# A hybrid decoder layer on one core: gates and branch products turned to token-major, and two late loads cut into pieces

## The chip, the cores and the metric

One core of one Trainium2 chip. The metric is the device time of one launch in microseconds, lower is better. The kernel before was run three times: median 1575.02 us (1573.05 to 1575.83).

## What is computed

The layer reads 256 tokens of width 2048. One input projection feeds three branches (dilated attention A, chunked gMLP B, an S5 state-space layer C) and three gates per channel; each branch is projected back to 2048, weighted by its gate, summed, and projected once more; a SwiGLU feed-forward part follows. Cut to what matters here:

```python
proj = x @ w_in + b_in                       # x: 256 x 2048
q, k, v, zb, uc, gl = split(proj)            # gl: 3 x 2048 gate columns
ya = ...                                     # attention, 512 wide
yb = ...                                     # gMLP, 768 wide
yc = gelu(s5(uc))                            # scan over 256 tokens
yc = yc * sigmoid(yc @ w_glu + b_glu)        # 768 wide
gates = sigmoid(gl.reshape(256, 3, 2048))
merged = gates[:, 0] * (ya @ w_pa) + gates[:, 1] * (yb @ w_pb) + gates[:, 2] * (yc @ w_pc)
x = layer_norm(ALPHA * x + merged @ w_o, ln1_g, ln1_b)
gate_f, up = split(x @ w_ffn_in)
f = (silu(gate_f) * up) @ w_ffn_out
out = layer_norm(ALPHA * x + f, ln2_g, ln2_b)
```

## The kernel before

**Number format.** Everything is float32 in and out. For TensorE a float32 value is split into a high part h (rounded to fp32r, by ScalarE: L280 for weights) and a low part l (the rest, by VectorE: L299), and a product is made of three: high by high, low by high, high by low.

**Units.** The work is a list of units, each one block of weights (up to 128 x 1024) with its load, its split, its matmuls (`mm`) and, at the end of a group, an eviction (`post`). A loop at the end of the kernel writes them out in order. Ahead of a unit's matmuls it splits the weights of later units and issues their loads on SyncE's queue (SP): four raw buffers, four split buffers, so that the loads run about four units ahead and the splits up to four. All weight loads, and most of the others, go through that one queue in this order. Between units it steps generators (`spawn`): the S5 set-up and scan, attention, gMLP, the turning of the feed-forward's rows (`turns`). `later` puts a small piece of work off by a unit.

**Feature-major stages** (`wide`, L80): the weights are the stationary operand, 128 output features at a time, and the activations are the moving one. `xT` holds per k 256 tokens of high and 256 of low part, so one matmul of 512 columns (L85: h by high and low) and one of 256 (L86: l by high) make a pair; 16 k make a tile of 128 features by 256 tokens. The two halves of the bank are added on eviction: ScalarE takes one half with the bias (L357, one value per partition), VectorE adds the other (L359).

**Token-major stages** (`tall`, L165; V, the output projection and the last projection): 128 tokens of activations are stationary, and 512 weight columns move, three matmuls (L171 to L173) per k and token half, and two banks (one per token half) for a group of 512 features.

**Gates and branch products before.** There are 16 feature tiles f and three branches b. `gates(f, b)` (L1312) is a wide group of two units; its eviction leaves 128 x 256 in `gx` (b of 0 or 1) or `g2` (b of 2), and a tanh a unit later (L887). `p_unit(f, b)` (L897) multiplies the branch's output by its projection, feature-major, with three matmuls of 256 columns per k (L906 to L908; 4, 6 and 6 k). Its eviction (L916, L918) multiplies by the gate and adds into `mab`, which is feature-major as well; for b of 2 the add is GpSimd's and the sum is split into `m` (high and low), as the output projection wants it: features on partitions.

**The scan.** Branch C's recurrence runs on GpSimd in two blocks of 128 time steps, four instructions a step (L586 to L589), on the tile X. The first block runs from about 100 us, the second beside the gates. `s5_out(1)` reads X on TensorE (L600); it is spawned at unit Y1, seven units before the first unit of the GLU (L1364).

**The last projection.** Its first unit's `before` is `ln2_load` (L1277): it starts the last `turns`, and issues four loads on SP: the residual rows `z` (two of 1 MB, kept in DRAM until then) and the norm weights `ln2w` (two of 1 MB, broadcast to the partitions). They go into the buffers that the seven-product stage's sums and `x1T` held.

The stages by time: input projection with q and k to 193 us, V to 259, gMLP inputs to 353, gates and products of branches 0 and 1 to about 611, the rest of the gates with the GLU to 711, the products of branch 2 to 746, output projection to 835, feed-forward to 1314, last projection to the end.

Of the kernel before, what the change touches and what calls it, by code (L numbers as in the profile page):

```python
# [32 lines left out]
def hybrid_layer(ctx: ExitStack, tc: tile.TileContext, d: dict, out: bass.AP):  # L33
# [24 lines left out]
    def s6(shape, dt, name):  # L58
        return sb.tile(shape, dt, tag="s6", bufs=11, name=name)
# [115 lines left out]
    def tall(srcs, kk, n, act, post, before=None, late=None, homes=()):  # L175
# [25 lines left out]
        for u, src in enumerate(srcs):  # L201
            last = u == len(srcs) - 1
            units.append(Unit(src, kk, n, mk(u), (lambda: post(st["ps"])) if last and not late else None,
                              before if u == 0 else None,
                              uses=1 if u < first_held else HL_BUFS if last else 0,
                              home=homes[u - first_held] if 0 <= u - first_held < len(homes) else None))

# [19 lines left out]
    def later(fn, wait=1):  # L227

        deferred.append([fn, wait])
# [16 lines left out]
    with tc.manual_schedule():  # L246
# [400 lines left out]
        def tables():  # L647
# [11 lines left out]
            for blk in range(4):  # L659
# [13 lines left out]
                yield  # L673
            s1 = dram.tile([8, L_TAB], F32, name="tab1")
# [198 lines left out]
        def gate(f, b):  # L873

            if b < 2:
                return big["gx"][:, f % 6, :]
            return big["g2", f // 6][:, f % 6, :]

        def post_gate(f, b):
# [16 lines left out]

        def p_unit(f, b, before=None):  # L897
            k0, k1 = ((0, 4), (4, 10), (10, 16))[b]
            st = {}

            def mm(h, l):
                st["ps"] = o = bank()[:, 0:256]
                for j in range(k1 - k0):
                    a = act_p(k0 + j)
                    hs, ls = h[:, j * 128:(j + 1) * 128], l[:, j * 128:(j + 1) * 128]
                    T.matmul(o, lhsT=hs, rhs=a[:, 0:256], start=j == 0, stop=False)  # L906
# [3 lines left out]
            def post():  # L910
                if (f, b) == (0, 0):
                    big["mab"] = sb.tile([128, 16, 256], F32, tag="t16", bufs=1, name="mab")
                if b == 2 and f % 3 == 0:
                    big["m", f // 3] = s6([128, 3, 512], F32R, f"m{f // 3}")
                g, m = gate(f, b), big["mab"][:, f, :]
                V.scalar_tensor_tensor(g if b else m, g, 1.0, st["ps"], op0=ALU.add, op1=ALU.mult)  # L916
                if b:
                    (G if b == 2 else V).tensor_tensor(m, m, g, op=ALU.add)  # L918
                if b == 2:
                    y = big["m", f // 3][:, f % 3, :]  # L920
                    later(lambda: copy_split(y[:, 0:256], y[:, 256:512], m))

            units.append(Unit(d["w_p"][f, :, k0:k1, :].rearrange("p k c -> p (k c)"), k1 - k0, 128, mm, post, before))
# [219 lines left out]
        def three(ps, a, h, l, start, stop):  # L1143
            T.matmul(ps, lhsT=a[0], rhs=h, start=start, stop=False)  # L1144
            T.matmul(ps, lhsT=a[1], rhs=h, start=False, stop=False)  # L1145
            T.matmul(ps, lhsT=a[0], rhs=l, start=False, stop=stop)  # L1146

# [129 lines left out]
        def ln2_load():  # L1277
            big["z"] = sb.tile([128, 2, D], F32, tag="t16", bufs=1, name="z")
            for t in range(2):
                nc.sync.dma_start(big["z"][:, t, :], big["zd"][:, t, :])  # L1280
            w = sb.tile([128, 2, D], F32, tag="t32", bufs=1, name="ln2w")
            spawn(turns(LAST))
            for i, nm in enumerate(("ln2_g", "ln2_b")):
                nc.sync.dma_start(w[:, i, :], d[nm].partition_broadcast(128))
            big["ln2"] = w
# [26 lines left out]
        def gates(f, b):  # L1312
            wide(wb(30 + f if b == 2 else 52 + 2 * f + b), 8, actx, post_gate(f, b))

# [5 lines left out]
        gates(0, 0)  # L1320
        for b in range(2):
            for f in range(16):
                if f < 15:
                    gates(f + 1, b)
                else:
                    gates(0, b + 1)
                p_unit(f, b, (lambda: finish(marks["gmlp"])) if (f, b) == (0, 1) else None)
        for f in range(1, 14):
            gates(f, 2)
# [3 lines left out]
        for f in range(14, 16):  # L1333
            gates(f, 2)
        for f in range(16):
            p_unit(f, 2)
# [225 lines left out]
```

## Time and profile before

| | |
|---|---|
| median of three runs | 1575.02 us |
| the profiled execution's own time | 1573.56 us |
| its span, first to last instruction | 1571.8 us |
| granted TensorE clock, mean | 0.997 |
| TensorE busy | 1546.5 us (98%), 8474 matmuls |
| VectorE / ScalarE / GpSimd busy | 1034.5 / 767.6 / 560.8 us |
| moved by DMA | 311.63 MB, mean 198 GB/s |

A row of a group reads: line, engine, operation, out<-in by the program's names, shapes, count | busy us, mean ns of one | idle time before and what ended it. A row of the timeline: start us, duration us, engine, line, operation. Matmuls overlap in the records, since one starts before the end of the one before it is written down; the distance between two starts tells what one costs in a dense stretch. SPq rows are the issue of transfers, not the transfers.

### The profile page before, as it was taken

To read this page: it belongs to the slowest core of one execution; us is meant where nothing else is said; L and a number is where in the kernel's file an instruction comes from. 1 tells how busy PE (TensorE), PEld (TensorE's weight loads), DVE (VectorE), ACT (ScalarE), POOL (GpSimd) and SP (SyncE) were. 2 spreads that over 40 slices of the span, in tenths; PEclk is the share of its full clock that TensorE was granted. 3 is DMA by queue.
4 is the path that set the end of the run, shared out by engine and by line. 5 is a ranking of instruction groups with operands and counts; after the bars stand their busy time and mean duration, and the time that the engine had idled before them with its cause. 6 is when DMAs were issued, how large, how long until landed. Compare 5 with 4: busy or idle time off the path is not lost.

```text
span 1571.8 us, 23107 instructions
## 1 busy us (share of the span) xinstructions
PE 1546.5 (98%) x8474; PEld 1322.4 (84%) x8474; DVE 1034.5 (66%) x1318; ACT 767.6 (49%) x990; POOL 560.8 (36%) x1149
## 2 busy tenths in 40 slices
PE   8999999999999999999999999999999999999996
PEld 6888888898889998889889888888888887788885
DVE  5444555666856665469567788888888886555455
ACT  5454443556444444465444555555555554433342
POOL 7549999963999999303003000000000000000002
PEclk9999999999999999999999999999999999999998
DMA  7665565666665556556883666666666667666663
GB/s 277 202 222 187 188 217 174 179 184 188 209 193 185 187 188 199 187 155 182 292 286 131 195 190 212 187 193 197 189 199 189 189 201 290 207 195 192 197 190 105
DMA packets 168505, 311.63 MB, mean 198 GB/s; under 512 B 27631, under 2 KB 110063, under 8 KB 167624
## 3 DMA queue, kind: packets, MB, share of 16 engines
q1 hardware_dynamic: 168008, 307.92, 61.8%
q0 software_dynamic: 384, 2.25, 0.4%
q8 instruction: 66, 1.08, 0.3%
q14 instruction: 47, 0.39, 0.1%
HBM read 305.87 MB, written 7.63 MB: 199 GB/s over the span
## 4 chain that ended last, share of the span: by engine, by line
PE 91%; DVE 4%; DMA 2%; ACT 1%; issue 1%; POOL 0%; SPq 0%; POOLq 0%; ACTq 0%; DVEq 0%
PE ps_mm L85 21%; PE ps_mm L86 11%; PE ps_mm L171 8%; PE ps_mm L172 8%; PE ps_mm L173 8%; PE ps_sd L1146 5%; PE ps_sd L1144 4%; PE ps_mm L1144 4%; PE ps_mm L1146 4%; PE ps_sd L1145 4%; PE ps_mm L1145 4%; DVE wl L299 2%; PE ps_mm L908 1%; PE ps_mm L907 1%; PE ps_mm L906 1%; DMA raw<-in_w_f_dram 1%
## 5 line engine op out<-in xcount | busy, mean ns | idle before, releaser
L280 ACT ACTIVATE wh<-raw 128x1024 fp32r<-128x1024 f32 (+1 forms) x544 | 556.1, 1025 | 471.6 <-PE ps_mm L173 163.3
L299 DVE TENSOR_TENSOR wl<-raw,wh 128x1024 fp32r<-128x1024 f32 (+1 forms) x544 | 654.7, 1225 | 146.6 <-ACT wh L280 144.3
L85 PE MATMUL ps_mm<-xT,wh 128*128 128x512 f32 x1344 | 481.9, 401 | 7.7 <-ACT wh L62 5.7
L86 PE MATMUL ps_mm<-xT,wl 128*128 128x256 f32 x1344 | 378.8, 282 | 0.4 <-DVE wl L299 0.4
L85 PEld LDWEIGHTS ps_mm<-xT,wh 128*128 128x128 f32 x1344 | 253.9, 189 | 70.3 <-ACT wh L62 5.7
L987 POOL TENSOR_TENSOR z<-z,ln2w 128x512 f32<-128x512 f32 (+1 forms) x4 | 5.2, 1297 | 709.0 <-ACT z L986 709.0
L86 PEld LDWEIGHTS ps_mm<-xT,wl 128*128 128x128 f32 x1344 | 255.5, 190 | 1.3 <-DVE wl L299 0.7
L586 POOL TENSOR_TENSOR t<-s5keep,X 128x48 f32<-128x48 f32 x254 | 131.8, 519 | 50.7 <-ACT X L568 30.9
L589 POOL TENSOR_TENSOR X<-X,t 128x48 f32<-128x48 f32 x255 | 130.2, 511 | 20.0
L172 PE MATMUL ps_mm<-wl,h 128*128 128x512 f32 x340 | 132.4, 389 | 2.2 <-DVE wl L299 2.2
L171 PE MATMUL ps_mm<-wh,h 128*128 128x512 f32 x340 | 132.6, 390 | 0.4 <-ACT wh L280 0.4
L173 PE MATMUL ps_mm<-wh,h 128*128 128x512 f32 x340 | 132.3, 389 | 0.0
L588 POOL TENSOR_TENSOR X<-X,t 128x48 f32<-128x48 f32 x255 | 119.3, 468 | 32.8 <-ACT X L568 32.8
L587 POOL TENSOR_TENSOR t<-s5keep,X 128x48 f32<-128x48 f32 x254 | 111.7, 440 | 0.0
L357 ACT ACTIVATE tmp<-ps_mm,bcol 128x256 f32<-128x256 f32 x90 | 42.8, 475 | 137.9 <-PE ps_mm L86 137.7
L1144 PE MATMUL ps_sd<-wh,x1T 128*128 128x512 f32 x270 | 106.1, 393 | 0.0
L1144 PE MATMUL ps_mm<-wh,x1T 128*128 128x512 f32 x270 | 105.9, 392 | 0.0
L1146 PE MATMUL ps_sd<-wl,x1T 128*128 128x512 f32 x270 | 105.4, 390 | 0.0
L1146 PE MATMUL ps_mm<-wl,x1T 128*128 128x512 f32 x270 | 105.2, 390 | 0.0
L1145 PE MATMUL ps_mm<-wh,x1T 128*128 128x512 f32 x270 | 105.1, 389 | 0.0
L1145 PE MATMUL ps_sd<-wh,x1T 128*128 128x512 f32 x270 | 105.1, 389 | 0.0
L172 PEld LDWEIGHTS ps_mm<-wl,h 128*128 128x128 f32 x340 | 63.8, 188 | 15.6 <-DVE wl L299 2.6
(277 smaller groups left out, 2475.2 us busy)
## 6 DMA issues: line engine op xcount, KB each, us to landing
raw<-in_w_f_dram SPq DMA_DIRECT2D x264, 512.0 KB, 4.1
raw<-in_w_b_dram SPq DMA_DIRECT2D x164, 512.0 KB, 4.8
raw<-in_w_o_dram SPq DMA_DIRECT2D x32, 512.0 KB, 5.3
raw<-in_w_v_dram SPq DMA_DIRECT2D x24, 512.0 KB, 3.9
raw<-in_w_p_dram SPq DMA_DIRECT2D x32, 384.0 KB, 3.5
raw<-in_w_zv_dram SPq DMA_DIRECT2D x16, 384.0 KB, 3.6
tmp<-tab SPq DMA_DIRECT2D x64, 64.0 KB, 2.8
raw<-in_w_p_dram SPq DMA_DIRECT2D x16, 256.0 KB, 3.3
```

The lines of the kernel that those rows point to most:

```text
L85: T.matmul(ps, lhsT=h[:, j * 128:(j + 1) * 128], rhs=a, start=k == 0, stop=last, skip_group_check=True)
L86: T.matmul(ps[:, 0:256], lhsT=l[:, j * 128:(j + 1) * 128], rhs=a[:, 0:256], start=False, stop=last, skip_group_check=True)
L171: T.matmul(ps[:, :n], lhsT=ah, rhs=hs, start=k == 0, stop=False)
L172: T.matmul(ps[:, :n], lhsT=ah, rhs=ls, start=False, stop=False)
L173: T.matmul(ps[:, :n], lhsT=al, rhs=hs, start=False, stop=k == total - 1)
L280: A.activation(h[:, :m], raws[n][:, :m], AF.Copy)
L299: V.tensor_tensor(l[:, :m], raws.pop(n)[:, :m], h[:, :m].bitcast(F32), op=ALU.subtract)
L586: G.tensor_tensor(t1, keep[:, 0], prev, op=ALU.mult)
L589: G.tensor_tensor(cur, cur, t2, op=ALU.add)
L1144: T.matmul(ps, lhsT=a[0], rhs=h, start=start, stop=False)
L1145: T.matmul(ps, lhsT=a[1], rhs=h, start=False, stop=False)
L1146: T.matmul(ps, lhsT=a[0], rhs=l, start=False, stop=stop)
```

## The change

Gates and branch products become token-major, by groups n of four feature tiles (512 columns). `two_tiles` makes the units: a unit holds two k of four feature tiles, and each k and token half t takes three matmuls of 512 columns into one of two banks. `gates(n, b)` has 8 units, `p_units(n, b)` 2 or 3. The weight arrays are laid out as before, so a load takes four runs of two k (1 KB a run) where it took one run of eight.

The bias can no longer be a value per partition. `tables` turns the bias columns once on TensorE and writes them to DRAM as 96 rows (`rows`); the first unit of each gate group loads its four rows, broadcast to all partitions, into a free third of `gx` or a temporary; the eviction is one VectorE add per token half, and the tanh follows at once on ScalarE. `mab` is token-major, so after the products of branch 2 `turn_m` turns each 512 columns, four transposes per token half, on TensorE, and splits them into `m`. The order of the units of the third branch changes too: 24 gate units before the GLU (28 before), 8 after it between the first products. Y1 stays at seven units before the GLU.

`ln2_load` now only allocates; the loads go out in 12 pieces of 512 columns, one every three units, by the generator `load_late`.

```diff
+        def two_tiles(srcs, act, post, before=None):
...
+                    if u == 0:
+                        st["ps"] = [bank(), bank()]
+                    for t in range(2):
+                        for j in range(2):
+                            a = act(2 * u + j)
+                            hs, ls = (w.rearrange("p (f k c) -> p k f c", f=4, k=2)[:, j] for w in (h, l))
+                            three(st["ps"][t], (a[:, t * 128:(t + 1) * 128], a[:, 256 + t * 128:256 + (t + 1) * 128]),
+                                  hs, ls, (u, j) == (0, 0), (u, j) == (len(srcs) - 1, 1))
...
+        def gates(n, b):
...
+                row["b"] = tmp() if b == 2 else big["gx"][:, 2, :]
+                src = big["rows"][f0:f0 + 3 * fs + 1:fs, :]
+                nc.sync.dma_start(row["b"].rearrange("p (f c) -> p f c", f=4),
+                                  src.unsqueeze(0).to_broadcast([128, 4, 128]))
+
             def post(ps):
-                if (f, b) == (0, 0):
-                    big["gx"] = s6([128, 6, 256], F32, "gx")
-                if b == 2 and f % 6 == 0:
-                    big["g2", f // 6] = s6([128, 6, 256], F32, f"g2{f // 6}")
-                s = gate(f, b)
-                add_bias(ps, (C_G2 + f) if b == 2 else C_G01 + 2 * f + b, s)
-                later(lambda: A.activation(s, s, AF.Tanh, scale=0.5))
-            return post
+                for t in range(2):
+                    V.tensor_tensor(gate(n, b, t), ps[t], row["b"], op=ALU.add)
+                for t in range(2):
+                    A.activation(gate(n, b, t), gate(n, b, t), AF.Tanh, scale=0.5)
...
+        def p_units(n, b, before=None):
+            k0, k1 = ((0, 4), (4, 10), (10, 16))[b]
+
+            def post(ps):
+                if (n, b) == (0, 0):
+                    big["mab"] = sb.tile([128, 2, D], F32, tag="t16", bufs=1, name="mab")
+                for t in range(2):
+                    g, m = gate(n, b, t), big["mab"][:, t, n * 512:(n + 1) * 512]
+                    V.scalar_tensor_tensor(g if b else m, g, 1.0, ps[t], op0=ALU.add, op1=ALU.mult)
+                    if b:
+                        (G if b == 2 else V).tensor_tensor(m, m, g, op=ALU.add)
+                if b == 2:
+                    spawn(turn_m(n))
...
+        def turn_m(n):
+
+            for t in range(2):
+                yield
+                ps = bank("sd")
+                for f in range(4):
+                    T.transpose(ps[:, f * 128:(f + 1) * 128],
+                                big["mab"][:, t, (4 * n + f) * 128:(4 * n + f + 1) * 128], ident)
...
-        def p_unit(f, b, before=None):
...
-                    T.matmul(o, lhsT=hs, rhs=a[:, 0:256], start=j == 0, stop=False)
-                    T.matmul(o, lhsT=hs, rhs=a[:, 256:512], start=False, stop=False)
-                    T.matmul(o, lhsT=ls, rhs=a[:, 0:256], start=False, stop=j == k1 - k0 - 1)
...
+        def load_late():
+
+            for g in range(4):
+                c = slice(g * 512, g * 512 + 512)
+                pieces = [(big["z"][:, :, c], big["zd"][:, :, c])]
+                pieces += [(big["ln2"][:, i, c], d[nm][c].partition_broadcast(128))
+                           for i, nm in enumerate(("ln2_g", "ln2_b"))]
+                for dst, src in pieces:
+                    for _ in range(3):
+                        yield
+                    nc.sync.dma_start(dst, src)
...
+        for n in range(3):
+            units.extend(gates(n, 2))
         marks["glu"] = len(units)
         for c in range(6):
             glu(c)
-        for f in range(14, 16):
-            gates(f, 2)
-        for f in range(16):
-            p_unit(f, 2)
+        last = gates(3, 2)
+        units.extend(last[0:3])
+        units.extend(p_units(0, 2))
+        units.extend(last[3:6])
+        units.extend(p_units(1, 2))
+        units.extend(last[6:8])
+        for n in (2, 3):
+            units.extend(p_units(n, 2))
```

What stands in the engines' lists is shown at three places. On TensorE, where the first gate group ends and the first product of branch 0 begins, before (`ya` is attention's output, `wh` and `wl` the split weights, L564 is the scan's input product):

```order
L85 MATMUL ps_mm<-xT,wh 128x512
L86 MATMUL ps_mm<-xT,wl 128x256
L564 MATMUL ps_sd<-uT,bbT 128x128 x8
L906 MATMUL ps_mm<-ya_2804,wh 128x256
L907 MATMUL ps_mm<-ya_2804,wh 128x256
L908 MATMUL ps_mm<-ya_2804,wl 128x256
```

and after the change:

```order
L209 MATMUL ps_mm<-wh,xT 128x512
L210 MATMUL ps_mm<-wh,xT 128x512
L211 MATMUL ps_mm<-wl,xT 128x512
L209 MATMUL ps_mm<-wh,ya_2810 128x512
L210 MATMUL ps_mm<-wh,ya_2810 128x512
L211 MATMUL ps_mm<-wl,ya_2810 128x512
```

The pair of 512 and 256 columns and the three of 256 have become three of 512 in both.

On VectorE, around the first reads of the second scan block (L603 before, L608 after, which take what TensorE made of X), in the gates of the third branch. Before (L359 is the add that ends one gate tile, L299 a weight split; `g_7218` holds tiles 6 to 11):

```order
L359 TENSOR_TENSOR g_7218<-ps_mm,tmp_7317 128x256
L299 TENSOR_TENSOR wl<-raw,wh 128x1024 x2
L359 TENSOR_TENSOR g_7218<-ps_mm,tmp_7366 128x256
L299 TENSOR_TENSOR wl<-raw,wh 128x1024 x2
L359 TENSOR_TENSOR g_7218<-ps_mm,tmp_7415 128x256
L603 SCALAR_TENSOR_TENSOR uT<-uT,bcol,ps_sd 128x4x32 x2
```

and after (L932 ends a gate group for one token half, L304 is the split):

```order
L932 TENSOR_TENSOR g_6178<-ps_mm,tmp_6179 128x512 x2
L304 TENSOR_TENSOR wl<-raw,wh 128x1024 x8
L932 TENSOR_TENSOR g_6178<-ps_mm,tmp_6332 128x512
L932 TENSOR_TENSOR g_6331<-ps_mm,tmp_6332 128x512
L304 TENSOR_TENSOR wl<-raw,wh 128x1024 x2
L608 SCALAR_TENSOR_TENSOR uT<-uT,bcol,ps_sd 128x4x32 x2
```

Before, the read comes with the eleventh gate tile of the branch (22 units of the branch); after, two units into the third group (18 units).

On SP's queue, where the last projection begins, before (`raw` are weight loads):

```order
L262 DMA raw<-in_w_f_dram 128x1024 x7
L1280 DMA z<-zd 128x2048 x2
L1284 DMA ln2w<-in_ln_g_dram 128x2048
L1284 DMA ln2w<-in_ln_b_dram 128x2048
L262 DMA raw<-in_w_f_dram 128x1024 x81
```

and after:

```order
L267 DMA raw<-in_w_f_dram 128x1024 x10
L1343 DMA z<-zd 128x2x512
L267 DMA raw<-in_w_f_dram 128x1024 x3
L1343 DMA ln2w<-in_ln_g_dram 128x512
L267 DMA raw<-in_w_f_dram 128x1024 x3
L1343 DMA ln2w<-in_ln_b_dram 128x512
```

The four large transfers, with 81 weight loads behind them, have become twelve with three weight loads between each.

More of the change, by code (lines that the diff above doesn't have):

```diff
@@ L206, in tall, with three @@
                               home=homes[u - first_held] if 0 <= u - first_held < len(homes) else None))
+    def three(ps, a, h, l, start, stop):
+        T.matmul(ps, lhsT=a[0], rhs=h, start=start, stop=False)
+        T.matmul(ps, lhsT=a[1], rhs=h, start=False, stop=False)
+        T.matmul(ps, lhsT=a[0], rhs=l, start=False, stop=stop)
     tasks = []
@@ L673, in tables @@
                 yield
+            ps = bank("sd")
+            T.transpose(ps[0:96, 0:128], bcol, ident)
+            rows = tmp(128)[0:96]
+            V.tensor_copy(rows, ps[0:96, 0:128])
+            big["rows"] = dram.tile([96, 128], F32, name="rows")
+            nc.sync.dma_start(big["rows"], rows)
             s1 = dram.tile([8, L_TAB], F32, name="tab1")
@@ new lines, in four, with mk, mm @@
+        def four(w, f0, fs, k0):
+            return w[f0:f0 + 3 * fs + 1:fs, :, k0:k0 + 2, :].rearrange("f p k c -> p f (k c)")
+        def two_tiles(srcs, act, post, before=None):
+            st = {}
+            def mk(u):
+                def mm(h, l):
+                    if u == 0:
[6 more added lines that the diff above has]
+                                  hs, ls, (u, j) == (0, 0), (u, j) == (len(srcs) - 1, 1))
+                return mm
+            return [Unit(src, 8, 128, mk(u), (lambda: post(st["ps"])) if u == len(srcs) - 1 else None,
+                         before if u == 0 else None) for u, src in enumerate(srcs)]
@@ L895, in act_p @@
             return act_yc2(k - 10)
-        def p_unit(f, b, before=None):
[L898 to L906, printed above, removed]
-                    T.matmul(o, lhsT=hs, rhs=a[:, 256:512], start=False, stop=False)
-                    T.matmul(o, lhsT=ls, rhs=a[:, 0:256], start=False, stop=j == k1 - k0 - 1)
[L910 to L923, printed above, removed]
         def act_m(k):
@@ L1277, in ln2_load @@
         def ln2_load():
+            spawn(turns(LAST))
             big["z"] = sb.tile([128, 2, D], F32, tag="t16", bufs=1, name="z")
[L1279 to L1285, printed above, removed]
+            big["ln2"] = sb.tile([128, 2, D], F32, tag="t32", bufs=1, name="ln2w")
+            spawn(load_late())
+        def load_late():
[8 more added lines that the diff above has]
+                    nc.sync.dma_start(dst, src)
         def ln2_norm(eng, t, c, n, part=None):
@@ L1319, in hybrid_layer @@
         marks["a"] = len(units)
-        gates(0, 0)
         for b in range(2):
-            for f in range(16):
[L1323 to L1328, printed above, removed]
-            gates(f, 2)
+            for n in range(4):
+                units.extend(gates(n, b))
+                units.extend(p_units(n, b, (lambda: finish(marks["gmlp"])) if (n, b) == (0, 1) else None))
+        for n in range(3):
+            units.extend(gates(n, 2))
         marks["glu"] = len(units)
```

38 lines of the change are left out of this document (26 added, 12 removed).

## The prediction

> **What bounds the kernel now.** I read the page first, for the engines and the chain, then the chain in order of time, then windows stage by stage, then the timeline of TensorE for the distance from one matmul's start to the next.
>
> ```profile
> span 1571.8 us, 23107 instructions
> PEclk9999999999999999999999999999999999999998
> PE 91%; DVE 4%; DMA 2%; ACT 1%; issue 1%; POOL 0%; SPq 0%; POOLq 0%; ACTq 0%; DVEq 0%
> ```
>
> TensorE carries 91% of the chain at a full granted clock. A busy PE says little by itself, so I take starts. Here are a gate pair stage and a stage of 512-wide matmuls (start, duration):
>
> ```profile
> 443.15 0.40 PE L85 MATMUL ps_mm<-xT,wh 128*128 128x512 f32 x1
> ...
> 448.80 0.28 PE L906 MATMUL ps_mm<-ya,wh 128*128 128x256 f32 x1
> ...
> 450.25 0.40 PE L85 MATMUL ps_mm<-xT,wh 128*128 128x512 f32 x1
> ```
> ```profile
> 1399.83 0.39 PE L171 MATMUL ps_mm<-wh,h 128*128 128x512 f32 x1
> ...
> 1402.55 0.39 PE L171 MATMUL ps_mm<-wh,h 128*128 128x512 f32 x1
> ```
>
> Between the first two stand 16 pairs (512 and 256 columns): 5.65 us, 0.3531 each. Then 12 matmuls of 256 columns: 1.45 us, 0.1208 each. In the last fence are 12 matmuls of 512 columns: 2.72 us, 0.2267 each. Nothing waits inside these stretches, and the same distances repeat over nearly the whole span: the bound is how fast TensorE takes instructions. So a change is worth what it takes from TensorE's own list, as long as nothing else comes late.
>
> **Gates.** Before: 48 tiles x 16 pairs = 768 pairs x 0.3531 = 271.2 us. After: 12 groups x 96 matmuls of 512 columns = 1152 x 0.2267 = 261.2 us. The number of columns is the same (768 x 768 = 1152 x 512); only the number of instructions falls. **-10.0 us**, all on the path.
>
> **Branch products.** Before: 16 tiles x 16 k x 3 = 768 matmuls x 0.1208 = 92.8 us. After: 384 x 0.2267 = 87.1 us. **-5.7 us**, on the path.
>
> For both sums the Trainium skill, TensorE: Matmul & The Clock Gate, section "Wait — 56ns, not 53.3ns?", speaks against the change: a warm matmul takes its columns at 2.4 GHz plus about 2.5 ns whatever its width. By that the 768 instructions saved in all (384 and 384) are worth 1.9 us, an estimate, and the sum would be 13.8 us poorer. The rows above disagree: 226.7 ns at 512 and 120.8 at 256 leave about 15 ns that don't go with the columns, and the measurement decides.
>
> The new right operand is strided, four runs of 128 columns out of a 1024-wide tile. The seven-product stage reads its weights the same way, in four runs, and from loads cut in the same four pieces:
>
> ```profile
> 900.00:1300.00 400.00, 400.00 (x1798) 330.51 (x1797) 339.63 (x403) 212.40 (x246) 0.00 (x0) 1.00 0.63 195
> raw<-in_w_f_dram SPq DMA_DIRECT2D x264, 512.0 KB, 4.1
> raw<-in_w_b_dram SPq DMA_DIRECT2D x164, 512.0 KB, 4.8
> tmp<-in_b_v_dram SPq DMA_DIRECT2D x3, 256.0 KB, 4.3
> ```
>
> (columns of the first row: window, PE, weight load, DVE, ACT, POOL, clock, DMA share, GB/s.) PE is busy 400.00 of 400.00 us there at 195 GB/s. A new unit takes 512 KB per 12 matmuls, 2.72 us: 193 GB/s. So the shorter runs cost nothing that is seen; 160 of the 264 loads in the second row are of that kind and land in 4.1 us. The 12 bias rows add 256 KB each at the head of a group; I price them by the last row, 4.3 us to landing against 8 units x 2.72 = 21.8 us until the add. They stand on SP's queue ahead of one weight load, whose four buffers give 4 x 2.72 = 10.9 us. I take 0; if that cover went, up to 4.3 us a group.
>
> **Turning.** New on TensorE: 8 turns of four transposes, and one transpose of the bias columns early on. The LayerNorm does the same turn:
>
> ```profile
> 829.44 0.60 PE L1006 MATMUL ps_sd<-ident,z 128*128 128x128 f32 x4
> 829.79 0.48 PE L171 MATMUL ps_mm<-wh,m 128*128 128x512 f32 x1
> 830.11 0.40 PE L172 MATMUL ps_mm<-wl,m 128*128 128x512 f32 x1
> ```
>
> From 829.44 to 830.11 is 0.67 us, less the one matmul in it (0.23) 0.44. 8 x 0.44 + 0.1 = **+3.6 us**, on the path.
>
> **A wait at the turns.** The transposes stand one unit (2.72 us) behind the last product and need VectorE's product and GpSimd's add of the same 512 columns:
>
> ```profile
> L931 DVE SCALAR_TENSOR_TENSOR z<-tmp,ps_mm x8: 671/684/689, 769.1 to 835.1; 128x512 f32<-128x512 f32 x8
> L987 POOL TENSOR_TENSOR z<-z,ln x4: 1282/1298/1538, 828.6 to 843.1; 128x512 f32<-128x512 f32 x4
> L988 POOL TENSOR_TENSOR z<-z,ln x4: 1284/1620/2144, 830.2 to 844.5; 128x512 f32<-128x512 f32 x4
> ```
>
> 0.68 + 1.30 = 1.98 us at the middle of these rows, 0.69 + 2.14 = 2.83 at the worst, when a VectorE split runs beside the add. TensorE would wait 0 to about 0.5 us with the hand-overs, at four places; behind it stands the next weight unit. I take **+0.5 us**, ends 0 and 2. The second half of a turn comes a unit later and is covered. The split of the turned rows (ACT copies, DVE subtracts) replaces one that was there. The bias adds and tanh go from three small instructions per tile to two per 512 columns, on engines that are not the bound: free, and if VectorE were late, it would show as waits on wl.
>
> **The last rows and norm weights.** Before, four transfers of 1 MB go into SP's queue at the start of the last projection, ahead of the weight loads:
>
> ```profile
> 1319.87 0.47 SPq L1284
> 1320.76 13.30 DMA raw<-in_w_f_dram
> 1334.15 1.06 ACT wh L280
> ```
> ```profile
> 1334.49 0.39 PE L173 MATMUL ps_mm<-wh,h 128*128 128x512 f32 x1
> ...
> 1335.26 0.49 PE L171 MATMUL ps_mm<-wh,h 128*128 128x512 f32 x1 [0.39 <-ACT wh L280]
> ...
> 1338.00 0.50 PE L172 MATMUL ps_mm<-wl,h 128*128 128x512 f32 x1 [2.24 <-DVE wl L299]
> 1320.00:1340.00 20.00, 17.37 (x80) 13.77 (x79) 8.78 (x11) 7.45 (x10) 0.00 (x0) 1.00 0.84 342
> ```
>
> The weights behind them land after 13.30 us, and TensorE starts 0.55 and 2.51 us late (1335.26 for 1334.72; 1338.00 for 1335.49): 3.1 us lost. After, 12 pieces go out one per three units: 4 MB over 36 units x 2.72 = 98 us, 43 GB/s beside 193, in all 236, while the last row shows 342 moved. Each column block's rows land well before the residual that reads them (units 21, 43, 65, 87). I take the whole **-3.1 us**; ends -3.1 and 0, if the stall is only handed on to another load.
>
> **The scan, which comes due earlier.** `s5_out(1)` is put seven units before the GLU. It reads X, which GpSimd's scan fills:
>
> ```profile
> 643.27 0.32 POOL L589 TENSOR_TENSOR X<-X,t 128x48 f32<-128x48 f32 x1
> ```
> ```profile
> 666.57 1.01 PE ps_sd L600 x32
> ```
> ```profile
> 196.00:258.00 62.00, 57.23 (x122) 1.00 0.65 212
> 440.00:643.00 203.00, 187.40 (x400) 1.00 0.59 190
> ```
> ```profile
> 196.00:258.00 62.00, 29.17 (x23) 1.00 0.65 212
> 440.00:643.00 203.00, 93.41 (x79) 1.00 0.59 190
> ```
>
> Today 23 us lie between the scan's end, 643.6, and the first read, 666.6. From the first gate to that read TensorE now has 86 gate units (8 pairs each, 242.9 us) and 32 product units (16 x 12 and 16 x 18 matmuls, 58.0): 300.9. After the change it is 102 units of 2.72 = 277.5, since only 18 of 24 gate units of the last branch precede it where 22 of 28 did. TensorE comes at 666.6 - 23.4 + 0.1 = 643.3: the slack is used up to the last third of a microsecond. What then counts is the scan's pace. It is held up by VectorE's splits:
>
> ```profile
> 442.42 0.33 POOL L589 TENSOR_TENSOR X<-X,t 128x48 f32<-128x48 f32 x1
> 442.82 1.34 POOL L586 TENSOR_TENSOR t<-s5keep,X 128x48 f32<-128x48 f32 x1
> ```
> ```profile
> 442.43 0.42 DVE L359 TENSOR_TENSOR gx<-ps_mm,tmp 128x256 f32<-128x256 f32 x1 [3.24 <-ACT tmp L357]
> 442.77 1.22 DVE L299 TENSOR_TENSOR wl<-raw,wh 128x1024 fp32r<-128x1024 f32 x1
> ```
>
> Beside the split L299 (two inputs in SBUF) a step takes 1.34 us, beside the bias add L359 (one from PSUM) 0.33. The V stage (196 to 258) already has the new rhythm, one 1024-wide split per 2.72 us: 122 steps in 62 us, 1.97 per us, with the splits at 47% of VectorE; the gate stage now has 400 in 203, 1.97, at 46%. So the pace stays, and TensorE waits some 0.3 us; one step in fifty slower (1.93) makes it 4 us. I take **+1.0 us**, ends 0 and 7 (1.90 per us). The Trainium skill, SBUF — State Buffer, section "Who interferes with whom", says that a VectorE instruction with two SBUF inputs contends with GpSimd's reads and one with a single SBUF input does not. The two pairs of rows agree; by that rule the new 512-wide adds and products, which read PSUM, leave the pace alone.
>
> **Sum.** -10.0 - 5.7 + 3.6 + 0.5 - 3.1 + 1.0 = -13.7 us. The profiled execution took 1573.56 us (its span and 1.8 around it): 1559.9. The median of the runs shown, 1575.02, is 1.5 above it; on that footing 1561.3.
>
> **Rivals.** (a) *The scan is late by more than a few us.* The pace has nothing to spare, since TensorE now waits in order behind it. At 1.90 per us it ends 400/1.90 - 203 = 7.5 us later, at 1.86 12: 1568 to 1573. For: the slack is gone; against: the two equal paces. (b) *The same wait takes the whole gain: slower.* Place: the first matmul of `s5_out(1)`. Without a scan term the sum is -14.7; the scan's lateness passes that at 400/(203 + 14.4) = 1.84 per us, and at 1.80 (19 us late) the time is 1575.0 - 14.7 + 19.5 = 1579.8. It needs each split to hold the scan a fifth longer than in the V stage, or the wide in-place adds of the second branch to hold it as splits do. (c) *The width brings nothing*: a 512-wide matmul after the change costs what its columns cost in a pair, 0.3531 x 2/3 = 0.2354. Gates 0, products 384 x 0.2354 = 90.4, -2.4, turning +3.6, last rows -3.1, waits +1.5: -0.4, 1574.6. The change would then not do what its form promises. Against: L171 to L173 and the seven-product stage, both with a new weight load for each matmul, as here. The Trainium skill's rule on matmul cost, TensorE: Matmul & The Clock Gate, above, would end near the same place. (d) *Small waits at every group*: bias rows that land late, turns at their worst (2 us), weight loads behind the pieces: 3 to 6 us, 1564 to 1567. Against: covers of 10.9 and 21.8 us.
>
> **How the numbers follow.** Forecast 68%, with 1558 to 1564 as its own spread; (a) 13%, (b) 4%, (c) 4%, (d) 11%. The low end takes the waits at nothing (1575.0 - 15.2 = 1559.8) and the spread of the runs shown, 1573.05 to 1575.83: 1557. The high end goes through (d) and the nearer half of (a): 1569. About 0.2%, 3 us, is what a measurement tells here: faster means under 1571.9. Faster 0.91 (forecast, (d), nearly all of (a)), same 0.05 ((c) and the far end of (a)), slower 0.04.
>
> **What would show it.** Right: gate and product matmuls start 0.227 us apart; no wait of TensorE around the start of the last projection; X waited for by some 0 to 4 us, with TensorE's read near 643; waits on mab under 0.5 us each. Wrong: 0.235 us between starts, a TensorE wait on POOL of over 10 us, or weight loads that land later than 10 us in the gate stage.

## The result, and the profile after

The changed kernel took 1566.21 us, the median of 5 runs (1565.48 to 1566.79), against 1575.02 us for the kernel before beside it (5 runs, 1572.44 to 1575.83). The ratio is 0.9949, with a 95% interval of 0.9934 to 0.9963: 8.8 us faster by the medians, 8.0 by the ratio. The forecast was 1561.3, so 4.9 us of the expected gain are missing.

The page of the kernel after, its lines on the span, the clock and the chain:

```profile
span 1564.9 us, 21488 instructions
PEclk9999999999999999899999999999999999999998
PE 78%; POOL 16%; DVE 2%; issue 1%; ACT 1%; DMA 1%; POOLq 0%; SPq 0%; DVEq 0%; ACTq 0%
```

Two things are new. GpSimd stands in the chain with 16% where it had 0%, and one slice of the granted clock, the 17th (626 to 665 us), reads 8. Both point to one place: GpSimd's scan, and what TensorE does when it has to wait for it.

TensorE's timeline there (start, duration, engine, line, operation, and in brackets the idle time before it and what ended it):

```profile
643.70 0.39 PE L210 MATMUL ps_mm<-wh,xT 128*128 128x512 f32 x1
643.93 0.39 PE L211 MATMUL ps_mm<-wl,xT 128*128 128x512 f32 x1
648.39 1.94 PE L605 MATMUL ps_sd<-X,cm 128*32 128x128 f32 x32 [4.08 <-POOL X L594]
650.26 0.80 PE L209 MATMUL ps_mm<-wh,xT 128*128 128x512 f32 x1
650.85 0.63 PE L210 MATMUL ps_mm<-wh,xT 128*128 128x512 f32 x1
651.28 0.63 PE L211 MATMUL ps_mm<-wl,xT 128*128 128x512 f32 x1
...
653.37 0.39 PE L210 MATMUL ps_mm<-wh,xT 128*128 128x512 f32 x1
653.60 0.39 PE L211 MATMUL ps_mm<-wl,xT 128*128 128x512 f32 x1
...
654.62 1.08 PE L605 MATMUL ps_sd<-X,cm 128*32 128x128 f32 x32
640.00:666.00 26.00, 21.92 (x168) 16.98 (x167) 10.71 (x16) 10.83 (x15) 7.63 (x20) 0.87 0.33 105
```

TensorE has nothing left to do from 644.16 on (643.93 and the 0.23 that a matmul takes here) and starts on X at 648.39: 4.2 us of waiting. (The 4.08 in brackets counts from the recorded end of the matmul before.) Then its first 32 small matmuls take 1.94 us, though the same ones take 1.08 at 654.62, and the matmuls behind them start 0.43 us apart (650.85, 651.28) where 0.23 is usual (653.37, 653.60). In the last row the granted clock of that window is 0.87. From the first group of reads to the second it is 654.62 - 648.39 = 6.23 us. With a full clock it is 3.98 (two rows of an experiment below), so the slow clock costs 2.25 us on top of the wait: **6.4 us in one place**, as read off this timeline.

Elsewhere the timeline and the windows of the kernel after read as forecast (the last two rows: window, PE, weight load, DVE, ACT, POOL, clock, DMA share, GB/s):

```profile
640.07 0.39 PE L209 MATMUL ps_mm<-wh,xT 128*128 128x512 f32 x1
...
642.79 0.39 PE L209 MATMUL ps_mm<-wh,xT 128*128 128x512 f32 x1
499.99 0.39 PE L209 MATMUL ps_mm<-wh,yb 128*128 128x512 f32 x1
...
502.71 0.39 PE L209 MATMUL ps_mm<-wh,yb 128*128 128x512 f32 x1
703.11 0.60 PE L961 MATMUL ps_sd<-ident,mab 128*128 128x128 f32 x4
703.47 0.48 PE L209 MATMUL ps_mm<-wh,xT 128*128 128x512 f32 x1
703.78 0.40 PE L210 MATMUL ps_mm<-wh,xT 128*128 128x512 f32 x1
440.00:643.00 203.00, 203.00 (x897) 168.15 (x896) 118.35 (x111) 88.93 (x91) 187.88 (x387) 1.00 0.65 200
1320.00:1340.00 20.00, 20.00 (x94) 16.53 (x93) 9.93 (x11) 8.71 (x12) 0.00 (x0) 1.00 0.74 247
```

Gates and products both take 2.72 us per 12 matmuls (the first two pairs of rows). A turn costs 703.78 - 703.11 - 0.23 = 0.44 us, and no wait on mab stands before it. TensorE is busy for all of the 203 us of the gate stage and all of the 20 us where the last projection stalled. And GpSimd, which runs the scan, got through only 387 instructions in these 203 us, where it was 400 before.

### The profile page after: what moved, and what is told of

The parts are those of the page before. It is cut to its first block, busy times and chain, and to the rows that moved or that the text cites. A ratio compares the mean times of both kernels' runs of the same rounds, so it can differ in the third digit from the quotient of the medians.

```text
span 1564.9 us, 21488 instructions
## 1 busy us (share of the span) xinstructions
PE 1538.4 (98%) x7739; PEld 1287.6 (82%) x7739; DVE 1022.4 (65%) x1247; ACT 742.8 (47%) x902; POOL 566.5 (36%) x1141
## 3 DMA queue, kind: packets, MB, share of 16 engines
q0 software_dynamic: 384, 2.25, 0.4%
## 4 chain that ended last, share of the span: by engine, by line
PE 78%; POOL 16%; DVE 2%; issue 1%; ACT 1%; DMA 1%; POOLq 0%; SPq 0%; DVEq 0%; ACTq 0%
PE ps_mm L85 10%; PE ps_mm L171 9%; PE ps_mm L172 9%; PE ps_mm L173 9%; PE ps_mm L209 6%; PE ps_mm L211 6%; PE ps_mm L210 6%; PE ps_mm L86 5%; PE ps_sd L211 5%; PE ps_sd L209 4%; PE ps_sd L210 4%; POOL X L594 4%; POOL t L591 4%; POOL X L593 4%; POOL t L592 4%
## 5 line engine op out<-in xcount | busy, mean ns | idle before, releaser
L304 DVE TENSOR_TENSOR wl<-raw,wh 128x1024 fp32r<-128x1024 f32 (+1 forms) x528 | 644.1, 1239 | 206.0 <-ACT wh L285 202.7
L85 PE MATMUL ps_mm<-xT,wh 128*128 128x512 f32 x576 | 208.2, 405 | 7.1 <-ACT wh L62 5.5
L86 PE MATMUL ps_mm<-xT,wl 128*128 128x256 f32 x576 | 162.8, 283 | 0.0
L209 PE MATMUL ps_mm<-wh,xT 128*128 128x512 f32 x384 | 152.5, 397 | 0.0
L211 PE MATMUL ps_mm<-wl,xT 128*128 128x512 f32 x384 | 150.0, 391 | 0.0
L210 PE MATMUL ps_mm<-wh,xT 128*128 128x512 f32 x384 | 150.0, 391 | 0.0
L594 POOL TENSOR_TENSOR X<-X,t 128x48 f32<-128x48 f32 x255 | 132.2, 518 | 20.0
L85 PEld LDWEIGHTS ps_mm<-xT,wh 128*128 128x128 f32 x576 | 109.8, 191 | 35.3 <-ACT wh L62 5.5
L593 POOL TENSOR_TENSOR X<-X,t 128x48 f32<-128x48 f32 x255 | 123.9, 486 | 32.6 <-ACT X L573 32.6
L86 PEld LDWEIGHTS ps_mm<-xT,wl 128*128 128x128 f32 x576 | 110.2, 191 | 0.5 <-DVE wl L64 0.4
L209 PE MATMUL ps_sd<-wh,x1T 128*128 128x512 f32 x270 | 106.1, 393 | 0.0
```

What stands on the lines that cost most here:

```text
L85: T.matmul(ps, lhsT=h[:, j * 128:(j + 1) * 128], rhs=a, start=k == 0, stop=last, skip_group_check=True)
L86: T.matmul(ps[:, 0:256], lhsT=l[:, j * 128:(j + 1) * 128], rhs=a[:, 0:256], start=False, stop=last, skip_group_check=True)
L304: V.tensor_tensor(l[:, :m], raws.pop(n)[:, :m], h[:, :m].bitcast(F32), op=ALU.subtract)
L594: G.tensor_tensor(cur, cur, t2, op=ALU.add)
```

## Experiments

Theory: everything but the scan came out as forecast, and the missing time is the scan's lateness, made of the wait and of the slow clock behind it. Rivals: only the wait is lost and the slow matmuls belong to the reads of X; TensorE would lose the time elsewhere anyway; or the gates and products did not bring what was forecast. Each result is the median of the runs, and its ratio is to the kernel before on the same chip. The kernel after itself has 0.9949 in its first runs and 0.9955 in experiment 10, where it was run again beside the 22 matmuls of experiment 4 and beside experiments 11 and 12.

**1. The reads of X two units later.**

```diff
-        Y0, Y1 = marks["a"] - 4, marks["glu"] - 7
+        Y0, Y1 = marks["a"] - 4, marks["glu"] - 5
-                marks["y1"] = spawn(s5_out(1), 2)
+                marks["y1"] = spawn(s5_out(1), 3)
```

> The kernel after, with s5_out(1) put five units before the GLU in place of seven, at three steps a unit in place of two, so that its thirteen steps still end one unit before the GLU. TensorE then reaches X two units, 5.4 us, later: near 649.4 for a scan that ends at 648.3. Theory (the scan's lateness is what the forecast lacked: 4.2 us of waiting and some 2.2 us of a slow clock behind it): no wait of TensorE on X, no matmuls at 0.43 us behind it, and 1566.2 - 6.4 = 1559.8 us. Rival 1 (only the wait is lost; the slow matmuls belong to the reads of X themselves, whenever they come): 1566.2 - 4.2 = 1562.0, with the slow stretch still there. Rival 2 (three steps a unit crowd the vector engines, and the GLU waits for yc in place of X): a wait before the first GLU matmul as long as the one that went, 1565 to 1567.

Measured: 1561.88 us, ratio 0.9915 (0.990 to 0.993). TensorE's timeline of this run:

```profile
648.16 0.39 PE L211 MATMUL ps_mm<-wl,xT 128*128 128x512 f32 x1
650.48 2.76 PE L605 MATMUL ps_sd<-X,cm 128*32 128x128 f32 x48 [1.93 <-POOL X L594]
653.17 0.80 PE L209 MATMUL ps_mm<-wh,xT 128*128 128x512 f32 x1
...
656.50 1.52 PE L605 MATMUL ps_sd<-X,cm 128*32 128x128 f32 x48
```

The time is rival 1's number, but not for its reason: a wait of 1.93 us is still there. The scan now ends at 650.4, 2 us later; two more units were split beside it. The expectation had taken its end as fixed. It isn't: while TensorE works, VectorE splits weights, and the scan slows down (experiment 8 tests this). The slow stretch is still there too: 48 reads take 2.76 us, and the next 48, in the last row, 1.52.

**2. Two units earlier.**

```diff
-        Y0, Y1 = marks["a"] - 4, marks["glu"] - 7
+        Y0, Y1 = marks["a"] - 4, marks["glu"] - 9
```

> The kernel after, with s5_out(1) put nine units before the GLU in place of seven, at the same two steps a unit. TensorE reaches X near 638.5. While it waits no weights are split, and the scan runs at its undisturbed 1.31 us a step in place of some 2.1, so it ends some 2 us sooner, at 646.3. Theory (the scan bounds this place, and a wait brings a slow clock): the wait grows from 4.2 to about 7.8 us, the slow stretch behind it stays or grows, and the time is 1566.2 + 3.6 to + 5.4 = 1569.8 to 1571.6 us. Rival (the wait is only where lost time shows, and TensorE would lose it anyway elsewhere): 1566 as after.

Measured: 1568.92 us, ratio 0.9960 (0.9948 to 0.9973).

```profile
637.45 0.39 PE L211 MATMUL ps_mm<-wl,xT 128*128 128x512 f32 x1
646.78 1.94 PE L605 MATMUL ps_sd<-X,cm 128*32 128x128 f32 x32 [8.94 <-POOL X L594]
```

The wait doubled to 8.9 us and the time rose by 2.7 us, 1 us less than the low end of the theory. The scan ended at 646.7, 1.6 us sooner than in the kernel after; less was split beside it. Rival 2 (1566, as after) is out: the lowest of the five runs took 1567.68, so the longer wait is not made up elsewhere.

**3 and 4. The wait filled with work.** Matmuls whose result nothing reads stand ahead of the first read: 18 of them, then 22.

```diff
                 ps = bank("sd")
+                if (b, c) == (1, 0):
+                    for _ in range(18):
+                        T.matmul(ps, lhsT=xT[:, 0, 0:128], rhs=xT[:, 0, :], start=True, stop=True)
```

> The kernel after, with 18 matmuls of 512 columns whose result nothing reads put right ahead of s5_out(1)'s first read of X: 18 x 0.2267 = 4.1 us of work in the place of the 4.2 us of waiting. Theory (the idle time itself lowers the granted clock): the wait shrinks to about 0.2 us, the first reads of X take 1.0 us as they did before the change in place of 1.9, the matmuls behind them start 0.227 us apart in place of 0.43, and the time falls by about 2.2 us to 1564.0, though TensorE does more work. Rival (the slow stretch comes from the reads of X or from something that runs beside them): the slow stretch stays, 1566.2, or up to 1567 if the extra matmuls overshoot.

> The kernel after with 22 matmuls whose result nothing reads ahead of s5_out(1)'s first read of X, 5.0 us of work; with 18 the scan ended 0.6 us later than in the kernel after and left TensorE 1.4 us idle, the clock stayed full, and the time of the profiled run fell by 2.6 us while the median did not move. Theory (the idle time lowers the clock, worth 2.3 us between the first and the second read): no idle time over 1 us, first reads of 1.0 us, and a median 1.5 to 2.5 us below that of the unchanged kernel beside it. Rival (what the clock gives, the scan takes, since TensorE's work runs beside it): within 0.5 us of the unchanged kernel, with the clock full.

Measured: 1566.20 us, ratio 0.9940 (0.9928 to 0.9953) with 18, and 1566.27, ratio 0.9949 (0.9936 to 0.9961) with 22, where the unchanged kernel beside the latter took 1567.39 (below). TensorE with 18 (the first two rows) and with 22:

```profile
643.37 4.24 PE L604 MATMUL ps_sd<-xT 128*128 128x512 f32 x18
649.04 1.08 PE L608 MATMUL ps_sd<-X,cm 128*32 128x128 f32 x32 [1.43 <-POOL X L594]
...
644.26 5.15 PE L604 MATMUL ps_sd<-xT 128*128 128x512 f32 x22
649.94 1.08 PE L608 MATMUL ps_sd<-X,cm 128*32 128x128 f32 x32 [0.53 <-POOL X L594]
...
653.92 1.08 PE L608 MATMUL ps_sd<-X,cm 128*32 128x128 f32 x32
```

The clock is settled: without the idle time the same reads take 1.08 us in place of 1.94, and the second group follows the first after 653.92 - 649.94 = 3.98 us, not 6.23. So the slow stretch comes from the idle time, not from the reads (rival 1). But the time moved by 0 and by -1.1 us, less than 2.25, and the intervals overlap. In both runs TensorE started on X 5.7 us after its own work was done, against 4.2 in the kernel after and 5.6 when that was run again. So it is not resolved whether the scan took back what the clock gave, as the rival of the second expectation has it, or whether these runs only fell among the later ones. That the slow clock costs 2.25 us is read off the timeline; no run has saved that time by itself.

**5. Last rows and norm weights as before.** The old `ln2_load` in the kernel after, in place of the new one and `load_late`.

```diff
-            spawn(load_late())
+            for t in range(2):
+                nc.sync.dma_start(big["z"][:, t, :], big["zd"][:, t, :])
...
+            for i, nm in enumerate(("ln2_g", "ln2_b")):
+                nc.sync.dma_start(w[:, i, :], d[nm].partition_broadcast(128))
```

> The kernel after, with the last rows and the norm weights loaded as before the change: four transfers of 1 MB at the start of the last projection. Theory (the pieces are worth the 3.1 us that the forecast took): TensorE starts some 0.5 and 2.5 us late on two weight tiles between 1310 and 1335, and the time is 1566.2 + 3.1 = 1569.3 us. Rival (the stall is hidden or handed on once the stages ahead of it are shorter): 1566.2.

Measured: 1570.15 us, ratio 0.9971 (0.9959 to 0.9982), 3.9 us above the kernel after, 3.5 by the ratios.

```profile
1330.27 0.50 PE L171 MATMUL ps_mm<-wh,h 128*128 128x512 f32 x1
1333.00 0.50 PE L172 MATMUL ps_mm<-wl,h 128*128 128x512 f32 x1 [2.23 <-DVE wl L304]
```

The old stall is back, one start late by 2.5 us. The second late start that the expectation names, of some 0.5 us, is not in this trace.

**6. The reads of X three units later.** As experiment 1, with `marks["glu"] - 4` and four steps a unit.

> The kernel after, with s5_out(1) put four units before the GLU in place of seven, at four steps a unit. In the run with five units the scan ended at 650.4, 2 us later than in the kernel after, since two more units of weights were split beside it, and TensorE still waited 2.1 us. Theory (the scan's end follows TensorE by about two thirds of what TensorE is given, until it is done): TensorE comes near 651.1, the scan ends near 650.5 to 651, the wait is 0 to 0.5 us, no matmul behind it starts 0.43 us after another, and the time is 1566.2 - 6.4 = 1559.8 us, up to 1560.5. Rival (five units already gave all there is to have): 1561.9 as with five.

Measured: 1559.05 us, ratio 0.9911 (0.9897 to 0.9924).

```profile
653.20 1.95 PE L605 MATMUL ps_sd<-X,cm 128*32 128x128 f32 x64 [0.56 <-POOL X L594]
```

A wait of 0.56 us is left, and 64 reads take 1.95: the clock is full. The time is 0.8 us below the theory's 1559.8. TensorE came 1.4 us later than expected, and the scan ended at 653.2, where 650.5 to 651 stood.

**7. The gates ahead of the GLU.** All eight units of the last gate group before the GLU, and a product group behind it as cover.

```diff
-                units.extend(p_units(n, b, (lambda: finish(marks["gmlp"])) if (n, b) == (0, 1) else None))
-        for n in range(3):
+                if (n, b) != (3, 1):
+                    units.extend(p_units(n, b, (lambda: finish(marks["gmlp"])) if (n, b) == (0, 1) else None))
+        for n in range(4):
             units.extend(gates(n, 2))
...
-        last = gates(3, 2)
-        units.extend(last[0:3])
-        units.extend(p_units(0, 2))
-        units.extend(last[3:6])
-        units.extend(p_units(1, 2))
-        units.extend(last[6:8])
-        for n in (2, 3):
+        units.extend(p_units(3, 1))
+        for n in range(4):
             units.extend(p_units(n, 2))
```

> The kernel after in another order of units: all eight units of the last gate group stand before the GLU, and the three product units of the last group of the second branch behind it, as cover for the GLU's results. s5_out(1) keeps its seven units and two steps, so TensorE comes to X five units, 13.6 us, later, near 657, for a scan that ends near 651. Theory (the scan's lateness is the one thing that the change lost): no wait on X, a full clock behind it, 1566.2 - 6.4 = 1559.8 us. Rival (the later GLU leaves too little cover behind it): TensorE waits for yc2 or mab in the products of the last branch, 1561 to 1564 us.

Measured: **1558.46 us, ratio 0.9907 (0.9894 to 0.9921)**, beside 1573.59 for the kernel before: 15.1 us faster. With the kernel of experiment 6 it is the fastest of all; the two are not told apart. The page and the timeline:

```profile
span 1557.9 us, 21484 instructions
PE 95%; DVE 2%; DMA 1%; ACT 1%; POOL 0%; issue 0%; POOLq 0%; SPq 0%; DVEq 0%; ACTq 0%
656.95 0.39 PE L211 MATMUL ps_mm<-wl,xT 128*128 128x512 f32 x1
657.27 1.08 PE L605 MATMUL ps_sd<-X,cm 128*32 128x128 f32 x32
```
```profile
650.48 0.32 POOL L594 TENSOR_TENSOR X<-X,t 128x48 f32<-128x48 f32 x1
```

The scan ends at 650.8 and TensorE comes at 657: 6 us of slack, no wait, a full clock, and GpSimd is out of the chain.

**8. Splits doubled.** The subtraction that makes wl done twice in eight units of the gate stage.

```diff
+            r = raws.pop(n)
+            for _ in range(2 if marks["a"] + 40 <= n < marks["a"] + 48 else 1):
-            V.tensor_tensor(l[:, :m], raws.pop(n)[:, :m], h[:, :m].bitcast(F32), op=ALU.subtract)
+                V.tensor_tensor(l[:, :m], r[:, :m], h[:, :m].bitcast(F32), op=ALU.subtract)
```

> The kernel after, with the subtraction that makes wl done twice, with the same result, for eight units in the middle of the gate stage. VectorE has room for it. Theory (every split of a weight unit holds the scan up by 0.91 to 0.95 us, whenever it falls beside it, and the number of splits ahead of the scan's end sets when it ends): the scan ends 8 x 0.93 = 7.4 us later, near 655.7, less what it gains in the longer wait; TensorE waits 10 to 11.5 us in place of 4.2, and the time is 1566.2 + 6 to + 7.5 = 1572 to 1573.7 us. Rival 1 (the pace is set by TensorE's or the transfers' traffic, not by VectorE's splits): the scan's end and the time stay, 1566.2. Rival 2 (a VectorE that is late with wl stalls TensorE on weights): waits on wl in the gate stage.

Measured: 1573.82 us, ratio 1.0003 (0.9994 to 1.0012): the whole gain of the change is gone. TensorE's timeline, GpSimd's window (its busy time and instructions, clock, DMA share, GB/s), and the window of the doubled line on VectorE:

```profile
655.17 1.94 PE L607 MATMUL ps_sd<-X,cm 128*32 128x128 f32 x32 [11.96 <-POOL X L596]
440.00:643.00 203.00, 188.66 (x366) 1.00 0.66 202
440.00:643.00 203.00, 104.30 (x82) 1.00 0.66 202
```

Undisturbed, the scan does a step of four instructions in 1.31 us, as here in the kernel after, while TensorE waits:

```profile
644.48 0.31 POOL L591 TENSOR_TENSOR t<-s5keep,X 128x48 f32<-128x48 f32 x1
645.79 0.31 POOL L591 TENSOR_TENSOR t<-s5keep,X 128x48 f32<-128x48 f32 x1
```

Seven more splits in the gate window (82 for 75) took 387 - 366 = 21 instructions from the scan, which is 6.9 us, about 1 us for each split. The wait grew to 12 us. No weight came late. So VectorE's splits set the scan's pace.

**9. Turns at once.** The first half of a turn right behind the last product matmul.

```diff
             for t in range(2):
-                yield
+                if t:
+                    yield
                 ps = bank("sd")
```

> The kernel after, with the first half of each of the four turns put right behind the last product matmul in place of one unit, 2.72 us, later. Theory (the unit between them is what hides VectorE's product and GpSimd's add, which the forecast put at 1.98 to 2.83 us): TensorE waits 2 to 3 us on mab at each of the four turns, 8 to 12 us in all, perhaps with a slow clock behind each, and the time is 1574 to 1580 us. Rival (the weights queued behind are ready, the wait is short or is made up): under 1568.

Measured: 1568.83 us, ratio 0.9972 (0.9961 to 0.9983).

```profile
700.26 0.39 PE L211 MATMUL ps_mm<-wl,yc 128*128 128x512 f32 x1
701.42 0.66 PE L962 MATMUL ps_sd<-ident,mab 128*128 128x128 f32 x4 [0.77 <-POOL mab L948]
```

Each of the four turns starts 701.42 - 700.26 - 0.23 = 0.93 us late, 3.7 us in all and not 8 to 12; by the ratios the time rose by 3.6. The expectation forgot that the bank of the first token half gets its last matmul six matmuls (1.36 us) before the unit ends. So the product and the add take 1.36 + 0.93 = 2.3 us, and in the kernel after the cover is 2.72 + 1.36 = 4.1: no wait, as seen.

**10. The kernel after again.**

> The kernel after, unchanged, beside the next three on one chip, as what they are measured from: 1566 us, ratio to before 0.995.

Measured: 1567.39 us, ratio 0.9955 (0.9941 to 0.9969).

```profile
642.45 0.39 PE L211 MATMUL ps_mm<-wl,xT 128*128 128x512 f32 x1
648.28 1.94 PE L605 MATMUL ps_sd<-X,cm 128*32 128x128 f32 x32 [5.44 <-POOL X L594]
```

Its wait on X was 5.44 us where the first run of it had 4.08. The scan ended at the same time as there (648.3), but TensorE came 1.5 us sooner. So the wait of one and the same kernel differs by more than 1 us from run to run.

**11. Halves.** Each 512-wide matmul of `two_tiles` as two of 256, save the first and last of an accumulation.

```diff
+                                n = 4 if s or e else 2
+                                for q in range(0, 4, n):
+                                    T.matmul(st["ps"][t][:, 128 * q:128 * (q + n)], lhsT=lhs, rhs=w3[:, q:q + n, :],
+                                             start=s, stop=e)
```

> The kernel after, with the gate and product matmuls of 512 columns cut into two of 256, except the first and the last of each accumulation: 1440 matmuls become 2880, with the same columns and the same result. Theory (the gain of the gates and products is the price of an instruction, 2 x 0.1208 - 0.2267 = 0.0149 us for each one saved): 1440 x 0.0149 = 21.5 us more on TensorE, of which 17 ahead of the scan's end, so that the wait on X and the slow clock behind it go (-6.4): 1566.2 + 15.1 = 1581.3 us. Rival (the fixed price is about 2.5 ns a matmul, as the Trainium skill, TensorE: Matmul & The Clock Gate, section "Wait — 56ns, not 53.3ns?", states): 3.6 us more on TensorE, 2.9 of it ahead of the scan, part of which the wait gives back: 1567 to 1569 us.

Measured: 1576.75 us, ratio 1.0013 (1.0004 to 1.0021).

```profile
500.40 0.64 PE L911 MATMUL ps_mm<-wh,xT 128*128 128x256 f32 x4
500.87 0.40 PE L911 MATMUL ps_mm<-wl,xT 128*128 128x256 f32 x2
501.12 0.65 PE L911 MATMUL ps_mm<-wh,xT 128*128 128x256 f32 x4
```

Six matmuls of 256 take 501.12 - 500.40 = 0.72 us, 0.120 each, so a saved instruction is worth 2 x 0.120 - 0.2267 = 13 ns, not 15. Against experiment 7, where nothing waits either, the ratios differ by 0.0106, 16.7 us: 11.6 ns for each of the 1440. So a matmul of half the width costs more than half, and the width is a part of what made the gates and products faster. By the 2.5 ns a matmul of the Trainium skill (TensorE: Matmul & The Clock Gate, section "Wait — 56ns, not 53.3ns?") it would have been 3.6 us, an estimate; the measurement decides.

**12. The loads alone, in the kernel before.** The new `ln2_load` and `load_late`, nothing else.

> The kernel before, with only the loads of the last rows and the norm weights cut into the twelve pieces. Theory (the stall at the start of the last projection is worth its 3.1 us by itself): TensorE busy throughout 1310 to 1340, and 3.1 us less than before, ratio 0.998, 1571.9 on a median of 1575.0. Rival (the pieces meet weight loads elsewhere in the last projection): ratio 1.000, with TensorE waiting on weights between 1340 and 1430.

Measured: 1569.49 us against 1573.92, ratio 0.9973 (0.9962 to 0.9985): 4.4 us, with 3.1 inside the interval (2.4 to 6.0). The window of the old stall:

```profile
1320.00:1340.00 20.00, 20.00 (x94) 16.53 (x93) 11.07 (x13) 8.72 (x12) 0.00 (x0) 1.00 0.75 238
```

TensorE is busy throughout, as in the kernel after.

## Why the forecast was right, and where its size was off

- **Gates -10.0, products -5.7: held.** Both stages start a matmul every 0.2267 us, and rival (c) needed 0.2354. The fixed part is 12 to 13 ns an instruction (experiment 11), a little under the 15 of the forecast. For the 768 instructions saved that is 9 to 10 us of the 15.7. Most of the rest, 4.3 us, lies in the old pair of the gates: it took 0.3531 us, where one matmul of 512 and one of 256 columns, each among its like, take 0.2267 + 0.1208 = 0.3475 (768 x 0.0056). The forecast's sum contains this, since it took the pair's price as measured. Why the pair cost more no run shows.
- **Turns +3.6: held.** 0.44 us for four transposes, the very number taken from the LayerNorm.
- **Wait at the turns +0.5: nothing.** The cover is a unit and a half, not one (experiment 9).
- **Last rows and norm weights -3.1: held, within the noise.** The time is 3.9 us more when they are undone (experiment 5, whose trace shows 2.5 of it) and 4.4 less when they are done alone (12).
- **These together** are -10.0 - 5.7 + 3.6 - 3.1 = -15.2 us. Experiment 7 is the changed kernel, in another order, with no wait on the scan: 15.1 us faster than before (12.4 to 16.7 by its interval).
- **The scan +1.0: this is the step that failed, in its size.** The arrival was right (forecast 643.3, measured 644.2 and, in experiment 10, 642.7). What failed is "So the pace stays, and TensorE waits some 0.3 us": the pace fell from 1.97 to 387/203 = 1.91 instructions per us and the wait was 4.2 us. The forecast had written 4 us down for "one step in fifty slower" (its steps there are single instructions), and then did not choose it. It also had no price for the clock behind a wait: 2.25 us by the timeline. Together that is +6.4 where +1.0 stood. -15.2 + 6.4 = -8.8 us, which is what the medians show.

That the time still lies in the range owes something to the rivals that the range took in. 1566.2 is outside the forecast's own spread of 1558 to 1564. By its number it belongs to (d), by its mechanism to (a).

Why the pace fell: GpSimd's window above (387 instructions) and the splits' own window in the kernel after (VectorE's busy time on the split's line) are to be set beside the 400 and the 93.41 us of the kernel before. Behind it stand two in-place adds on VectorE and the scan instructions beside them:

```profile
440.00:643.00 203.00, 94.50 (x75) 1.00 0.65 200
```
```profile
505.00 0.73 DVE L948 TENSOR_TENSOR mab<-mab,gx 128x512 f32<-128x512 f32 x1
506.36 0.77 DVE L948 TENSOR_TENSOR mab<-mab,gx 128x512 f32<-128x512 f32 x1
```
```profile
505.14 0.77 POOL L592 TENSOR_TENSOR t<-s5keep,X 128x48 f32<-128x48 f32 x1
506.66 0.64 POOL L591 TENSOR_TENSOR t<-s5keep,X 128x48 f32<-128x48 f32 x1
```

I took, for every scan instruction in these 203 us, its time over that of the undisturbed ones (0.31 to 0.32), and booked it to the VectorE instruction beside it. Before it is 68.9 us, after 73.1. Of the 4.2 us more, 2.5 are the splits', now all 1024 wide at 0.95 each and packed closer in time since TensorE asks for them sooner. 1.6 are the second branch's in-place adds (beside them the scan's instructions take 0.77 and 0.64 us in the last two rows): 16 adds of 256 columns before held the scan up by 1.5 us in all, 8 of 512 after by 3.1. The V stage has none of them. Four instructions take 1.31 us undisturbed, so 4.2 us are 13 instructions, and 400 - 387 = 13. This booking is argued from the trace; that splits move the scan's end is shown by experiment 8.

The V stage was a poor witness. Its 62 us hold 23 splits of about 1 us of scan each, so one split more or less at its edge is 1.5% of its pace, and the answer hung on 1%. In the runs of the changed kernel and its variants the same 62 us hold 121 to 125 instructions. Rival (a) is the mechanism that came, at 4.7 us of lateness (648.3 for 643.6) where it began to count at about 7. Rival (b)'s pace came in experiment 8, 366/203 = 1.80: but the time was 1573.8, not the 1579.8 that the forecast gave for it. The scan ended 11.5 us late and not 19, since a scan that is waited for has no splits beside it and runs its last steps undisturbed. The mechanism of (d) is not seen: TensorE is never idle in the gate stage, and no turn waits.

The Trainium skill, SBUF — State Buffer, section "Who interferes with whom", says that a VectorE instruction with two SBUF inputs contends with GpSimd's reads. The trace agrees: beside the in-place adds, which have two SBUF inputs as the splits do, scan instructions of 0.31 us take 0.64 and 0.77. The forecast had the rule, but its sum counted only the splits under it; the adds stand in its rival (b) alone.

## What to carry to other kernels

When a change takes the last slack from another engine's work, give that work its slack back in the same change: three units later, or another order, were worth some 7 us here, nearly half of what the change could bring. Where an engine is held up by VectorE's weight splits, a faster TensorE can slow it down, because the same splits fall into less time; take its pace from the trace as a price per split (here about 1 us), not as a rate from another stage. And price a wait of TensorE at more than its length: by the timeline, 4.2 us of waiting cost 6.4 here.

## What was not expected of the hardware

After idle times of 0.53, 0.56 and 1.43 us TensorE went on at full speed (32 reads in 1.08 us, 64 in 1.95). After 1.93, 4.08, 5.44, 8.94 and 11.96 us it ran at about half: reads of 1.94 us for 32, matmuls 0.43 us apart, for 3.3 us (after 1.93) to 5.9 us (after 5.44); in the kernel after from 648.39 to 653.4, in experiment 2 from 646.78 to 650.9. The stretch does not grow with the wait: after 11.96 us it was 5.4, after 4.08 it was 5.0. The Trainium skill, TensorE: Matmul & The Clock Gate, section "What's actually happening", puts the drop to half speed after an idle window of about 3.4 us, and the return after as long a busy one. The half speed agrees, and the slow stretches are about as long as that or longer. The idle time does not agree: here 1.93 us were enough.

A scan step of four instructions is hardly slowed by TensorE itself: it took 1.34 us beside the 22 extra matmuls and 1.31 while TensorE was idle. In both places VectorE had nothing to do; what held the scan up elsewhere, as far as these traces show, were VectorE's instructions.
